# A hybrid attention and mixture-of-experts block: a longer hand-written order, with four small pieces of work moved in it

## The chip, the cores and the metric

The kernel runs on one core of a Trainium2 chip. The metric is the device time of one execution in microseconds (us). The engines are called PE (TensorE), DVE (VectorE), ACT (ScalarE), POOL (GpSimd) and SP (SyncE, which here issues nearly all DMAs). Each engine takes its instructions strictly in program order.

## What is computed

One decoder layer on 256 tokens of width 1024, in float32. A mixer comes first (an input projection, two kinds of attention, gates, an output projection), then a layer norm, then a mixture of 32 experts of which each token takes four.

```python
proj = x @ w_in + b_in                       # 4120 columns: q, k, v, gates
y_a = banded_attention(...)                  # sliding window 128, with sinks
y_b = nsa_attention(...)                     # g0*compressed + g1*selected + g2*window
gate_a, gate_b = jnp.split(jax.nn.sigmoid(merge_g), 2, axis=-1)
merged = gate_a * (y_a @ w_branch_a) + gate_b * (y_b @ w_branch_b)
h = layer_norm(alpha * x + merged @ w_out, ln1_g, ln1_b)
logits = h @ w_router + b_router             # top 4 of 32 experts, softmax
# each expert: act = clamped_swiglu(xb @ w_gate_up[e] + b_gate_up[e]); act @ w_down[e] + b_down[e]
out = layer_norm(alpha * h + moe(h), ln2_g, ln2_b)
```

## The kernel before

**The stages.** The mixer's input projection is 32 *units* of 128 columns. Unit 0 to 15 make queries, keys and values, unit 16 to 31 the merge gates (tiles `M`, `mg`). A unit is 24 matmuls (units 0 and 1: 8), because each operand is split into a high and a low part (`mm3`, lines 256 to 258), and runs as two *half units* of 12; half unit `h` belongs to unit `h // 2`. After the units come eight products with the branch weights (`pb`), the output projection (`po`), the router, and then the 32 experts, whose weights (12 MB each) stream from memory into some twelve 2 MB buffers. SP issues the next load into a buffer as soon as the readers of what it held are done.

**The order between half units.** After each half unit the main loop calls the steps that the table `PLAN` names for it. For an attention pair `br r` (two heads; branch 0, 1, 2) `S` makes the scores (PE, DVE, then ACT's exponentials for branches 1 and 2), `N` normalises them (DVE, then four operations on POOL, line 693), `T` transposes them (PE, then copies `pT` on ACT, line 705), and `V` multiplies with the values and adds to `yB` (line 727; for branch 2 ACT and DVE then make the high and low part `yhl`). `cp0` to `cp3` add the compressed branch, which reads `pcT`, the transposed compressed probabilities that step `ct` makes (`pct` on PE, a copy on ACT, line 604). `mlp`, `gelu` and `ck` make the compressed keys: a product `phid`, a copy `hp_`, a product `phidT`, a chain of six small operations on `cu` (lines 541 to 547, one of them ACT's tanh) and the product `pkc`. `h` and `l` make the high and low part of a unit's weights (`w_j`), two to three units ahead; the low part reads the high part. PE's transposes take their results from a pool of two PSUM buffers named `t`, PE's scores and `cp` products from three named `s`.

**Other steps.** `bl`, `bsa` to `bsd`, `bw` and `br` load the experts' biases, split them into three bfloat16 parts in a tile `bt` (lines 488 and 490, DVE and ACT), store them to a buffer `bd` in memory and load them again as rows `bparts`. `rw` scales the router's weights (lines 775 and 776, four DVE operations), sums them over partitions on PE (`pgb`, line 778) and adds the sums to constants. `sig` applies the sigmoid, in place, to the gates of the units from 16 to `SIG0 - 1`, which were copied out of PSUM without it; from unit `SIG0` on the copy applies it. `vt0` transposes a value tile.

**Who sets the order.** PE and SP run in program order throughout. DVE, ACT and POOL run in program order up to half unit `MAN_END`; what comes behind that is put in order by a scheduler, which may also take an instruction ahead. At half unit `END_H` (42) the attention's tiles are released, and expert weights load over them.

Of the kernel before, what the change touches and what calls it, by code (L numbers as in the profile page):

```python
# [10 lines left out]
F32 = mybir.dt.float32  # L11
# [9 lines left out]
P = 128  # L21
# [3 lines left out]
E = 32  # L25
# [7 lines left out]
GELU_C = math.sqrt(2.0 / math.pi)  # L33
NRA, NRB = 3, 3
WARM = 6
NWS, NSB, AHEAD, SIG0 = 3, 6, 2, 20
POOL_PART = {6: 'h', 8: 'h', 9: 'h', 10: 'h', 11: 'h', 12: 'h', 13: 'h', 14: 'h', 15: 'h', 16: 'h', 17: 'h', 18: 'h', 19: 'h', 20: 'h', 21: 'h', 22: 'h', 23: 'h', 24: 'h', 25: 'h', 27: 'l', 28: 'l', 30: 'l', 38: 'l'}
SIDE_R = "right"
LOADS, LOADS2 = 6, 11
# [3 lines left out]
MAN = 2  # L43
TWO = 4
LATE = range(6, 22)
MAN_END = 42
LN_ROWS = {9 + i: (0, i) for i in range(4)} | {20 + i: (1, i) for i in range(4)}
E_RES = 13
PLAN = {7: 'gates', 8: 'sinks blkz', 9: 'c1 gsum h6 l6', 10: 'S00 h7 l7 E00', 11: 'S01 h8 E01 N00', 12: 'vt0 S02', 13: 'N01 T00 E02 l8 h9', 14: 'N02 V00 T01 S03 bias1', 15: 'h10 V01 T02 E03', 16: 'l9 V02', 17: 'N03 l10 bl', 18: 'T03 h11 l11', 19: 'V03 blocks',
# [3 lines left out]
        43: 'sig', 44: 'sel'}  # L53
PRE = {26: 1, 43: 1, 45: 1, 48: 1, 64: 1, 71: 1, 72: 2, 73: 3}


# [8 lines left out]
def tile_block(ctx: ExitStack, tc: tile.TileContext, a, out):  # L65
# [4 lines left out]
    cp = ctx.enter_context(tc.tile_pool(name="cp", bufs=1))  # L70
# [134 lines left out]
    def w_tile(name):  # L205
        nw[0] += 1
        return ps_w.tile([P, 512], F32, tag=f"w{nw[0] % 2}", name=name)
# [8 lines left out]
    pp = er.enter_context(tc.tile_pool(name="pp", bufs=2, side=SIDE_R))  # L216
# [333 lines left out]
    hid = mp.tile([P, 2, 4, 32], F32, name="hid")  # L550
# [61 lines left out]
    def cmp_pv(r):  # L612
        t = ps_s.tile([P, 512], F32, tag="s", name=f"yc{r}")
        q_ = slice(32 * r, 32 * r + 32)
        for g in range(2):
            PE.matmul(t[64 * g:64 * g + 64, :S], vc[q_, 64 * g:64 * g + 64], y_["pcT"][q_, g, :], start=True, stop=True,
                      tile_position=(32 * r, 64 * g))
        DVE.tensor_tensor(y_["B"][:, r, :], y_["B"][:, r, :], t[:, :S], ALU.add)
# [145 lines left out]
    def sigmoids():  # L764
        for k in sorted((k for k in mg if 16 + k[0] + 2 * k[1] < SIG0), key=lambda k: (k[1], k[0])):
            ACT.activation(mg[k], mg[k], AF.Sigmoid)

    def router_weights():

        wb = pp.tile([P, 384], F32, tag="s", bufs=NSB, name="wb")[:, :256].rearrange("p (j e) -> p j e", j=NJ)  # L770
        gb = pp.tile([P, 384], F32, tag="s", bufs=NSB, name="gb")[:, :2 * E]
        for i in (1, 0):
            v = const[:, C_L1 + 8 * i:C_L1 + 8 * i + 8].unsqueeze(2).to_broadcast([P, NJ, E])
            w_ = wb if i else wr
            DVE.tensor_tensor(w_, wr, v, ALU.mult)
            DVE.tensor_reduce(gb[:, E * i:E * i + E], w_.rearrange("p j e -> p e j"), AX.X, ALU.add)
        t = ps_t.tile([P, 512], F32, tag="t", name="pgb")
        PE.matmul(t[:, :2 * E], ones, gb, start=True, stop=True)
        DVE.tensor_copy(wr_g, t[:, :E])
        DVE.tensor_tensor(br_b, br_b, t[:, E:2 * E], ALU.add)  # L780

    def sel():
# [4 lines left out]
    steps = {"bl": bias_load, "bsa": lambda: bias_split(0, "h"), "bsb": lambda: (bias_split(0, "l"), bias_split(1, "h")),  # L787
             "bsc": lambda: bias_split(1, "l"), "bsd": lambda: bias_split(2, "h"), "bw": bias_store, "br": bias_rows,
             "gates": gates, "gsum": gates_sum, "c1": load_c1, "sinks": sinks, "blkz": blocks_zero, "blocks": blocks, "mlp": mlp, "x": load_x, "gelu": gelu,
             "ck": ck, "hid": cmp_rows, "cv": cmp_v, "csm1": cmp_exp, "csm2": cmp_softmax, "ct": cmp_transpose, "rw": router_weights, "sig": sigmoids, "sel": sel}  # L790
    for b in range(3):
        steps[f"vt{b}"] = lambda b=b: v_transpose(b)
        steps[f"bias{b}"] = lambda b=b: load_T(b)
        for r in range(4):
            p = pairs[b][r]
# [4 lines left out]
    for r in range(4):  # L800
        steps[f"E0{r}"] = pa[r].exps
        steps[f"cp{r}"] = lambda r=r: cmp_pv(r)
    plan = {k: [steps[x] for x in v.split()] for k, v in PLAN.items()}
    h = 0
    for n in range(len(order)):
        for _ in unit(n):
            for f in plan.get(h, ()):
                f()
            if h == MAN_END:
                m0.close()  # L810
# [9 lines left out]
    for mt in range(8):  # L820
# [6 lines left out]
        t = w_tile(f"pb{mt}")  # L827
# [23 lines left out]
    lg = cp.tile([P, 2, 40], F32, name="lg")  # L851
    rep = cp.tile([P, 2, 40], F32, name="rep")
    sel = cp.tile([P, 2, E], F32, name="sel")
    gate = cp.tile([P, 2, E], F32, name="gate")
    posm = cp.tile([P, 2, E], F32, name="posm")
    v8 = cp.tile([P, 2, 8], F32, name="v8")
    sm = cp.tile([P, 2, 2], F32, name="sm")
# [363 lines left out]
    for e in range(E):  # L1221
        x, p = ex[e], (ex[e - 1] if e else None)
# [91 lines left out]
    with tc.For_i(0, nrun, 1) as e:  # L1314
# [13 lines left out]
        for tt in range(2):  # L1328
            t_ = slice(tt * P, (tt + 1) * P)
            for jj in range(2):  # L1330
                t = ps_w.tile([P, 512], F32, tag="w0", name=f"vht{tt}{jj}")
# [5 lines left out]
            for hf in range(2):  # L1337
# [7 lines left out]
                t = ps_w.tile([P, 512], F32, tag="w0", name=f"vt{tt}{hf}")  # L1345
# [116 lines left out]
```

## Time and profile before

| | |
|---|---|
| median of three runs | 1135.81 us (1134.64 to 1136.35) |
| profiled execution, its own time | 1137.99 us |
| its span, first to last instruction | 1136.2 us |
| mean granted PE clock | 0.988 |
| PE busy | 1067.2 us, 94% |
| DVE, ACT, POOL busy | 288.0, 212.2, 72.3 us |
| moved by DMA | 438.50 MB, mean 386 GB/s |

The span lies 1.8 us below the execution's own time, and that execution lies 2.2 us above the median of the runs. The page's chain of work follows only the last 0.1 us (a loop that runs zero times here), so the stages have to be read from tables by stretch, from timelines and from waits.

### The profile page before, as it was taken

The numbers are of one execution on the slowest core, as the hardware profiler recorded it, in microseconds if no ns is written. First come the engines' busy times: TensorE is split into PE (matmuls) and PEld (weight loads), VectorE is DVE, ScalarE is ACT, GpSimd is POOL, SyncE is SP. The second block draws the span as 40 slices with busy tenths as digits, with TensorE's granted clock in tenths as the row PEclk, the third lists the DMA queues.
The fourth block names the chain that finished last, engine by engine and source line by source line (L and its number), as shares of the span: only waits on it lengthen the run. The fifth ranks groups of instructions, "written<-read, shape, count | busy, mean of one in ns | idle before, by whom it ended". The sixth has DMA issues, their size and how long they took to land. (4 is left out here: it accounts for less than half of the span.)

```text
span 1136.2 us, 13443 instructions
## 1 busy us (share of the span) xinstructions
PE 1067.2 (94%) x5660; PEld 510.9 (45%) x5660; DVE 288.0 (25%) x695; ACT 212.2 (19%) x451; POOL 72.3 (6%) x113
## 2 busy tenths in 40 slices
PE   9999899999999999999999998998999988999995
PEld 7887798633434343434333433333433333333331
DVE  4885447412111111111121211111120202021213
ACT  3438344211101010111110101010111010001011
POOL 1444220000000000000000000000000000000000
PEclk9999899999999999999999999999999999999998
DMA  8654668799999999999999999999999999999993
GB/s 316 241 237 145 259 257 337 294 403 414 430 425 428 426 427 427 429 427 427 427 428 426 428 427 426 430 424 429 427 428 427 427 427 426 428 428 427 427 428 145
DMA packets 38288, 438.50 MB, mean 386 GB/s; under 512 B 4032, under 2 KB 6736, under 8 KB 9168
## 3 DMA queue, kind: packets, MB, share of 16 engines
q1 hardware_dynamic: 37888, 436.98, 92.2%
q8 instruction: 46, 0.75, 0.3%
q10 hardware_dynamic: 336, 0.62, 0.2%
q14 instruction: 18, 0.15, 0.0%
HBM read 435.92 MB, written 1.66 MB: 385 GB/s over the span
## 5 line engine op out<-in xcount | busy, mean ns | idle before, releaser
L1169 PE MATMUL g<-wg,xeM 128*64 128x512 f32 x1208 | 278.7, 598 | 2.9 <-DMA wg<-in_w_gu_dram 2.8
L1169 PEld LDWEIGHTS g<-wg,xeM 128*64 128x64 f32 x1208 | 82.4, 137 | 155.1 <-issue 136.1
L1196 PE MATMUL pd<-wd,wk 128*64 128x512 f32 x600 | 134.8, 595 | 16.8 <-DMA wd<-in_w_d_dram 16.7
L1169 PE MATMUL g<-wb,xeM 128*64 128x512 f32 x624 | 143.9, 596 | 1.2 <-DMA wb<-in_w_gu_dram 1.2
L1203 DVE COPY y<-pd 64x512 f32<-64x512 f32 x32 | 22.2, 694 | 432.8 <-ACT y L1202 432.8
L1196 PEld LDWEIGHTS pd<-wd,wk 128*64 128x64 f32 x600 | 43.0, 137 | 102.7 <-issue 79.8
L1149 DVE TENSOR_SCALAR gs<-g 128x512 f32<-128x512 f32 x32 | 22.1, 692 | 240.8 <-PE g L1169 240.8
L1169 PEld LDWEIGHTS g<-wb,xeM 128*64 128x64 f32 x624 | 42.6, 137 | 80.8 <-issue 72.7
L1196 PE MATMUL pd<-wb,wk 128*64 128x512 f32 x288 | 66.5, 608 | 9.2 <-DMA wb<-in_w_d_dram 9.1
L1202 ACT COPY y<-pd 64x512 f32<-64x512 f32 x32 | 18.5, 579 | 295.5 <-PE pd L1196 295.5
L256 PE MATMUL pu<-xhl,w_j 128*128 128x256 f32 x240 | 72.6, 302 | 0.3 <-ACT kT L436 0.2
L257 PE MATMUL pu<-xhl,w_j 128*128 128x256 f32 x240 | 69.2, 288 | 0.0
L258 PE MATMUL pu<-xhl,w_j 128*128 128x256 f32 x240 | 69.1, 288 | 0.0
L1124 PEld LDWEIGHTS px<-wk,h_tok 128*128 128x128 f32 x480 | 55.8, 191 | 24.3 <-issue 12.2
L1083 POOL TENSOR_SCALAR wk<-const,posm 128x64 f32<-128x64 f32 x30 | 12.8, 446 | 796.3 <-PE pst L1138 792.2
L1124 PE MATMUL px<-wk,h_tok 128*128 128x128 f32 x480 | 61.5, 281 | 0.0
L1145 PE MATMUL yac<-y,wk 128*128 128x512 f32 x128 | 59.2, 605 | 0.7 <-ACT y L1202 0.7
L1185 ACT COPY wk<-pa 128x512 f32<-128x512 f32 x31 | 18.2, 587 | 196.9 <-PE pa L1184 185.6
L256 PEld LDWEIGHTS pu<-xhl,w_j 128*128 128x128 f32 x240 | 47.3, 197 | 4.0 <-issue 2.7
L1169 PE MATMUL g<-wp,xeM 128*64 128x512 f32 x208 | 48.4, 596 | 0.0
L257 PEld LDWEIGHTS pu<-xhl,w_j 128*128 128x128 f32 x240 | 47.4, 198 | 0.0
L258 PEld LDWEIGHTS pu<-xhl,w_j 128*128 128x128 f32 x240 | 47.3, 197 | 0.1
(246 smaller groups left out, 1018.6 us busy)
## 6 DMA issues: line engine op xcount, KB each, us to landing
wg<-in_w_gu_dram SPq DMA_DIRECT2D x72, 2048.0 KB, 38.5
wb<-in_w_gu_dram SPq DMA_DIRECT2D x38, 2048.0 KB, 34.5
wd<-in_w_d_dram SPq DMA_DIRECT2D x36, 2048.0 KB, 39.1
wb<-in_w_d_dram SPq DMA_DIRECT2D x16, 2048.0 KB, 39.1
wp<-in_w_gu_dram SPq DMA_DIRECT2D x12, 2048.0 KB, 38.2
w<-in_w_in_dram SPq DMA_DIRECT2D x14, 1024.0 KB, 7.6
wp<-in_w_d_dram SPq DMA_DIRECT2D x7, 2048.0 KB, 39.1
wg<-in_w_gu_dram SPq DMA_DIRECT2D x7, 1024.0 KB, 10.3
```

The source lines that it names most:

```text
L256: PE.matmul(o_, wh, xh, start=start, stop=False)
L257: PE.matmul(o_, wh, xl, start=False, stop=False)
L258: PE.matmul(o_, wl, xh, start=False, stop=stop)
L1083: (DVE if tt else POOL).tensor_scalar(oh[:, tt, k, :], iota[:, :CAP], posm[:, tt, e + k:e + k + 1], None, ALU.is_equal)
L1124: PE.matmul(t[:, k * P:(k + 1) * P], h_tok[:, tt, j * P:(j + 1) * P], oh[:, tt].rearrange("p k s -> p (k s)"), start=(tt == 0), stop=(tt = ...
L1145: PE.matmul(yac[tt][o_], st[:, tt * P:(tt + 1) * P], y2[:, o_, :], start=first, stop=last)
L1149: DVE.tensor_scalar_min(g_, gate_, LIMIT)
L1169: PE.matmul(self.g[b][64 * hf:64 * hf + 64, :], xes[e][:, j, :], w[:, 1024 * b + 512 * hf:1024 * b + 512 * hf + 512], start=False, stop=(j ...
L1185: ACT.copy(self.aT, t)
L1196: PE.matmul(d[64 * o_:64 * o_ + 64, :], self.aT[:, P * j + 64 * hf:P * j + 64 * hf + 64], w[j // 2][:, 1024 * (j % 2) + 512 * o_:1024 * (j ...
L1202: ACT.copy(y2[k, 0, :], d[:CAP])
L1203: DVE.tensor_copy(y2[k, 1, :], d[CAP:])
```

## The change

`MAN_END` goes from 42 to 50, so that the hand-written order holds for eight half units more, and with it nine things change place:

- `sig` from half unit 43 to 48, for eight gates rather than four (`SIG0` 24), so units 20 to 23 are copied out without the sigmoid;
- `bsb`, `bsc`, `bsd`, `bw` and `br` from half units 21, 22, 26, 28 and 35 to 35, 36, 37, 38 and 42;
- `rw` is cut in two: the DVE part, `rwd`, at half unit 41, the sum on PE, `rwp`, at 47 (before both were at 42). Its result now stands in the tile `gate`, which lives to the end, and not in a tile of the attention's pool;
- `ct` ahead of `S21`, and `vt0` behind `S02`, within their half units.

```diff
-NWS, NSB, AHEAD, SIG0 = 3, 6, 2, 20
+NWS, NSB, AHEAD, SIG0 = 3, 6, 2, 24
...
-MAN_END = 42
+MAN_END = 50
...
-        20: 'h12 l12 bsa', 21: 'bsb mlp', 22: 'h13 bsc gelu', 23: 'ck l13', 24: 'S10 h14', 25: 'h15 l14 N10 hid', 26: 'S11 bsd', 27: 'T10 l15 N11 h16 S12',
...
-        43: 'sig', 44: 'sel'}
...
+        20: 'h12 l12 bsa', 21: 'mlp', 22: 'h13 gelu', 23: 'ck l13', 24: 'S10 h14', 25: 'h15 l14 N10 hid', 26: 'S11', 27: 'T10 l15 N11 h16 S12',
...
+        44: 'sel', 47: 'rwp', 48: 'sig'}
...
+    gate = cp.tile([P, 2, E], F32, name="gate")
+    gb = gate.rearrange("p t e -> p (t e)")
+
     def router_weights():
 
         wb = pp.tile([P, 384], F32, tag="s", bufs=NSB, name="wb")[:, :256].rearrange("p (j e) -> p j e", j=NJ)
-        gb = pp.tile([P, 384], F32, tag="s", bufs=NSB, name="gb")[:, :2 * E]
         for i in (1, 0):
             v = const[:, C_L1 + 8 * i:C_L1 + 8 * i + 8].unsqueeze(2).to_broadcast([P, NJ, E])
             w_ = wb if i else wr
             DVE.tensor_tensor(w_, wr, v, ALU.mult)
             DVE.tensor_reduce(gb[:, E * i:E * i + E], w_.rearrange("p j e -> p e j"), AX.X, ALU.add)
+
+    def router_sums():
         t = ps_t.tile([P, 512], F32, tag="t", name="pgb")
         PE.matmul(t[:, :2 * E], ones, gb, start=True, stop=True)
         DVE.tensor_copy(wr_g, t[:, :E])
```

On ACT, at step `S21`, before. The scheduler had taken the four sigmoids of `sig` (line 766) ahead to between the pairs of branch 2, each with a table load on either side (`M` is a gate, `sb_1` the pair's scores, `pct` the transposed compressed probabilities):

```order
L705 COPY pT_3_0_1165<-t_3_0_1161 128x384
L705 COPY pT_3_1_1171<-t_3_1_1167 128x384
L766 ACT_TABLE_LOAD
L766 ACTIVATE M_72<-M_72 128x256
L679 ACT_TABLE_LOAD
L679 ACTIVATE sb_1_0_1207,su_1_1206<-sb_1_0_1207,st_1_1205 128x256
...
L604 COPY pcT<-pct 128x512
L459 ACTIVATE M_74<-pu_1180,const 128x256
```

and now, at the same place:

```order
L705 COPY pT_3_0_1161<-t_3_0_1157 128x384
L705 COPY pT_3_1_1167<-t_3_1_1163 128x384
L604 COPY pcT<-pct 128x512
L679 ACTIVATE sb_1_0_1210,su_1_1209<-sb_1_0_1210,st_1_1208 128x256
...
L459 ACTIVATE M_74<-pu_1176,const 128x256
```

The sigmoid and both table loads are gone from here, and the copy of `pcT` stands ahead of the exponentials. The eight sigmoids with one table load stand behind the high part of unit 26's weights, ahead of the copy of unit 24's gate.

On DVE, at steps `mlp`, `gelu` and `ck`, before (`bt` is the biases' tile, `hp_`, `cx` and `cu` are the small chain's):

```order
L432 TENSOR_SCALAR qT_665<-pu_684,pk 128x256
L490 TENSOR_TENSOR bt<-bt 128x768
L531 COPY hp__749<-phid 128x128
L490 TENSOR_TENSOR bt<-bt 128x768
L541 COPY cx<-phidT 128x60
L542 TENSOR_TENSOR cu<-cx 128x60
```

and now:

```order
L432 TENSOR_SCALAR qT_666<-pu_685,pk 128x256
L531 COPY hp__748<-phid 128x128
L541 COPY cx<-phidT 128x60
L542 TENSOR_TENSOR cu<-cx 128x60
L543 TENSOR_TENSOR cu<-cu,cx 128x60
```

The two passes over the biases are gone from ahead of the chain. They stand in the pairs of branch 2 now: one behind `N21`'s two operations and ahead of `S22`'s, one behind `cp0` and the low part of unit 20's weights, and the cast `bsd` ahead of `S23`'s.

On DVE, at step `V23` (the last pair), before (`w_j22` and `w_j23` are units 22's and 23's weights, `yB` and `yhl` as above, `const_66` holds the router's weights):

```order
L234 TENSOR_TENSOR w_j22_1431<-w10_681,w_j22_1431 128x1024
L727 TENSOR_TENSOR yB_751<-yB_751,y2_2_1447 128x256
L234 TENSOR_TENSOR yhl_167<-yB_751,yhl_167 128x256
L234 TENSOR_TENSOR w_j23_1481<-w10_681,w_j23_1481 128x1024
L727 TENSOR_TENSOR yB_751<-yB_751,y2_3_1497 128x256
...
L775 TENSOR_TENSOR wb_1507<-const_66 128x256
L776 TENSOR_REDUCE gb_1508<-wb_1507 128x32
L775 TENSOR_TENSOR const_66<-const_66 128x256
L776 TENSOR_REDUCE gb_1508<-const_66 128x32
L779 COPY const_66<-pgb_1513 128x32
```

and now:

```order
L234 TENSOR_TENSOR w_j22_1431<-w10_682,w_j22_1431 128x1024
L727 TENSOR_TENSOR yB_750<-yB_750,y2_2_1447 128x256
L234 TENSOR_TENSOR yhl_167<-yB_750,yhl_167 128x256
L777 TENSOR_TENSOR wb_1480<-const_66 128x256
L778 TENSOR_REDUCE gate_170<-wb_1480 128x32
L777 TENSOR_TENSOR const_66<-const_66 128x256
L778 TENSOR_REDUCE gate_170<-const_66 128x32
L234 TENSOR_TENSOR w_j23_1486<-w10_682,w_j23_1486 128x1024
L727 TENSOR_TENSOR yB_750<-yB_750,y2_3_1502 128x256
```

The router's four operations stand ahead of unit 23's low part and of `V23`'s addition. PE's product `pgb` stood right behind `V23`'s products, ahead of the second half of unit 21; now it stands behind unit 23. On SP the store to `bd` and the load of `bparts` move behind the last two loads of the input weights, and `bparts` behind the load of `x` as well.

## Rows read from the trace of the kernel before

**Rows 1.** Stretches: us; PE, PEld, DVE, ACT, POOL busy (count); PE clock, DMA share, GB/s.

```profile
128.00:216.00 88.00, 87.70 (x658) 82.56 (x658) 47.40 (x87) 37.92 (x54) 13.43 (x10) 0.98 0.78 309
216.00:260.00 44.00, 43.60 (x222) 17.35 (x220) 10.22 (x33) 6.75 (x13) 0.00 (x0) 1.00 0.96 386
...
400.00:1000.00 600.00, 566.07 (x2702) 219.67 (x2700) 98.50 (x213) 72.08 (x145) 8.55 (x20) 0.99 1.01 427
```

**Rows 2.** SP's waits, 216 to 262 us: waited for, us in total, times, longest.

```profile
SPq L83 <- PE g L1169: 26.7, 11, 8.3
```

**Rows 3.** Timeline of PE: start, us, line, names, shapes, count, [idle before, releaser].

```profile
33.32 0.44 PE L472 MATMUL pvt<-const,vt 128*128 128x128 f32 x2 [1.28 <-ACT vt L440]
...
63.75 0.40 PE L561 MATMUL pkc<-cu,pk 128*64 128x15 f32 x4 [2.11 <-DVE cu L547]
...
99.18 0.30 PE L700 MATMUL t<-const,sb 128*128 128x128 f32 x1 [1.98 <-ACT pcT L604]
...
111.78 0.33 PE L700 MATMUL t<-const,sb 128*128 128x128 f32 x1
...
121.72 1.50 PE L718 MATMUL y<-pT,V 128*64 128x256 f32 x4 [2.17 <-ACT pT L705]
...
127.05 0.66 PE L778 MATMUL pgb<-gb,const 128*128 128x64 f32 x2 [3.40 <-DVE gb L776]
```

**Rows 4.** Stretches at and behind three of these gaps, columns as in rows 1.

```profile
63.75:67.00 3.25, 3.25 (x18) 2.99 (x18) 1.55 (x3) 0.00 (x0) 0.00 (x0) 0.50 0.41 169
...
99.18:102.60 3.42, 3.42 (x28) 2.74 (x28) 0.58 (x5) 2.93 (x6) 1.60 (x4) 1.00 1.02 343
121.71:131.90 10.19, 6.77 (x31) 6.01 (x32) 4.07 (x10) 1.22 (x3) 1.05 (x1) 0.50 0.83 328
```

**Rows 5.** Timeline of DVE at the small chain.

```profile
60.10 0.96 DVE L490 TENSOR_TENSOR bt<-bt 128x768 f32<-128x768 f32 x1 [0.70 <-ACT bt L488]
...
61.73 1.09 DVE L544 SCALAR_TENSOR_TENSOR cu<-cu,cx 128x60 f32<-128x60 f32 x1
```

**Rows 6.** Timeline of POOL.

```profile
61.72 1.05 POOL L226 TENSOR_SCALAR w_j<-w 128x1024 fp32r<-128x1024 f32 x1 [3.33 <-DVE cu L543]
...
108.56 1.64 POOL L693 TENSOR_SCALAR sb<-sb,su 128x256 f32<-128x256 f32 x4 [2.77 <-DVE su L690]
115.42 1.63 POOL L693 TENSOR_SCALAR sb<-sb,su 128x256 f32<-128x256 f32 x4 [5.22 <-DVE su L690]
117.02 2.07 POOL L226 TENSOR_SCALAR w_j<-w 128x1024 fp32r<-128x1024 f32 x2
...
141.25 2.40 POOL L232 TENSOR_TENSOR w_j<-w,w_j 128x1024 fp32r<-128x1024 f32 x1 [6.15 <-ACT w_j L228]
```

**Rows 7.** ACT, 92 to 117 us, grouped: count, busy us, mean ns, idle before.

```profile
L766 ACT ACT_TABLE_LOAD x4 | 5.1, 1283 | 0.1
...
L766 ACT ACTIVATE M<-M 128x256 f32<-128x256 f32 x4 | 1.7, 419 | 0.0
```

**Rows 8.** Timeline of ACT.

```profile
121.20 0.85 ACT L705 COPY pT<-t 128x384 f32<-128x384 f32 x2
...
139.76 0.48 ACT L461 ACTIVATE M<-pu,const 128x256 f32<-128x256 f32 x1 [1.47 <-PE pu L258]
...
142.64 0.48 ACT L461 ACTIVATE M<-pu,const 128x256 f32<-128x256 f32 x1 [1.47 <-PE pu L258]
```

**Rows 9.** Timeline of DVE at the last pair.

```profile
118.10 2.06 DVE L234 TENSOR_TENSOR w_j<-w,w_j 128x1024 fp32r<-128x1024 f32 x1 [2.85 <-POOL w_j L226]
120.08 0.41 DVE L727 TENSOR_TENSOR yB<-yB,y 128x256 f32<-128x256 f32 x1
...
124.92 0.42 DVE L775 TENSOR_TENSOR wb<-const 128x256 f32<-128x256 f32 x1
...
126.32 0.58 DVE L776 TENSOR_REDUCE gb<-const 128x32 f32<-128x256 f32 x1
```

**Rows 10.** DMA issues, whole span: KB each, us from issue to landing.

```profile
bd<-bt SPq DMA_DIRECT2D x1, 576.0 KB, 15.2
```

More of the change, by code (lines that the diff above doesn't have):

```diff
@@ L45 @@
 LATE = range(6, 22)
-MAN_END = 42
+MAN_END = 50
 LN_ROWS = {9 + i: (0, i) for i in range(4)} | {20 + i: (1, i) for i in range(4)}
 E_RES = 13
-PLAN = {7: 'gates', 8: 'sinks blkz', 9: 'c1 gsum h6 l6', 10: 'S00 h7 l7 E00', 11: 'S01 h8 E01 N00', 12: 'vt0 S02', 13: 'N01 T00 E02 l8 h9', 14: 'N02 V00 T01 S03 bias1', 15: 'h10 V01 T02 E03', 16: 'l9 V02', 17: 'N03 l10 bl', 18: 'T03 h11 l11', 19: 'V03 blocks',
[3 rows of a table removed]
-        43: 'sig', 44: 'sel'}
+PLAN = {7: 'gates', 8: 'sinks blkz', 9: 'c1 gsum h6 l6', 10: 'S00 h7 l7 E00', 11: 'S01 h8 E01 N00', 12: 'S02 vt0', 13: 'N01 T00 E02 l8 h9', 14: 'N02 V00 T01 S03 bias1', 15: 'h10 V01 T02 E03', 16: 'l9 V02', 17: 'N03 l10 bl', 18: 'T03 h11 l11', 19: 'V03 blocks',
[3 rows of a table added]
+        44: 'sel', 47: 'rwp', 48: 'sig'}
 PRE = {26: 1, 43: 1, 45: 1, 48: 1, 64: 1, 71: 1, 72: 2, 73: 3}
@@ L789, in tile_block @@
              "gates": gates, "gsum": gates_sum, "c1": load_c1, "sinks": sinks, "blkz": blocks_zero, "blocks": blocks, "mlp": mlp, "x": load_x, "gelu": gelu,
-             "ck": ck, "hid": cmp_rows, "cv": cmp_v, "csm1": cmp_exp, "csm2": cmp_softmax, "ct": cmp_transpose, "rw": router_weights, "sig": sigmoids, "sel": sel}
+             "ck": ck, "hid": cmp_rows, "cv": cmp_v, "csm1": cmp_exp, "csm2": cmp_softmax, "ct": cmp_transpose, "rwd": router_weights, "rwp": router_sums, "sig": sigmoids, "sel": sel}
     for b in range(3):
@@ L853, in tile_block @@
     sel = cp.tile([P, 2, E], F32, name="sel")
-    gate = cp.tile([P, 2, E], F32, name="gate")
     posm = cp.tile([P, 2, E], F32, name="posm")
```

4 rows, old and new, of the table PLAN are left out of this document.

## The prediction

> **What bounds the kernel now.** I read the table by stretches first, because the chain of work says nothing here. From 400 to 1000 us the DMA engines are busy throughout at 427 GB/s and PE has 34 us of idle time in 600: the weight stream sets the pace. From 128 to 216 us it is the other way round: PE is busy 87.70 of 88.00 us and DMA stands at 0.78 [rows 1]. The two meet at 216 us. There SP's waits say who lets the stream go: eleven loads, 26.7 us in all, wait for PE's products `g` of the first expert to read a buffer empty [rows 2]. Up to then the buffers are full and the stream has to stand still; from then on the remaining bytes take a fixed time. So the end moves by as much as PE's arrival at the first expert moves, and since PE never waits between 128 and 216 us, that is PE's gain up to 128 us, one for one. What the experts do afterwards is the same program.
>
> Up to 128 us the timeline of PE shows five gaps at places that the change touches: 1.28 us at 33.32, 2.11 at 63.75, 1.98 at 99.18, 2.17 at 121.72 and 3.40 at 127.05 [rows 3]. Behind two of them the granted clock fell to 0.50, that is from 2.4 to 1.2 GHz: from 63.75 to 67.00 and from 121.71 to 131.90 us. Behind the 1.98 us at 99.18 it stayed at 1.00 [rows 4].
>
> **The change, part by part.**
>
> *The router's sum, `rw`.* `pgb` stands ahead of unit 21's second half, and PE waits 3.40 us for it [rows 3], because its four DVE operations (two of 0.42, two of 0.58) can begin only when DVE has done `V23` [rows 9]. Now the product is asked for behind unit 23, and the operations stand ahead of `V23`'s: **3.4** gained. Cover for the moved part: its 2.0 us on DVE delay unit 23's low part, which is wanted 1.5 units after `V23`, 4.3 us at the 2.88 us from one gate copy to the next [rows 8]. Nothing is lost.
>
> *The last pair's gap, 2.17 us.* PE waits for ACT's `pT`, done from 121.20 on [rows 8]. Backwards from it: ACT waits for `V22`'s addition on DVE (120.08), which stands behind unit 22's low part (118.10, 2.06), which needs its high part from POOL (117.02), which stands behind `N23`'s normalisation (115.42, 1.63) [rows 6, 9]. `N23` follows the pair's exponentials, ahead of which a table load of 1.28 us goes [rows 7]. So the chain comes 1.28 us earlier against PE, and up to 0.8 more if the low part is no longer slowed by POOL, which works beside it. The gap falls to between 0.1 and 0.9; I take 0.6, gain **1.6** (bounds 1.3 and 2.1).
>
> *The clock behind it.* In 121.71 to 131.90 PE was busy 6.77 us at half rate [rows 4]; at full rate that is **3.4** less. It comes if both gaps ahead go (bounds 0 and 3.4). I take all of it: 1.98 us of idle time did not cost the clock, and at most 0.9 is left.
>
> *`ct` ahead of `S21`.* The second transpose of `T20` needs the `t` buffer that `pct` holds until ACT has copied `pcT`, and that copy stood behind a sigmoid, two table loads and four exponentials. Now it stands ahead of them: the 1.98 us go, **2.0** (bounds 1.3, if ACT were still busy by one load's length, and 2.0). `S21` comes a product later, but its exponentials lose a table load, and that is more.
>
> *The biases' passes leave the small chain.* The pass at 60.10 held DVE for 0.96 us ahead of the chain that PE waits for. The chain then met POOL: an operation on 60 columns began at 61.73 and took 1.09 us, until POOL's high part (61.72, 1.05) had ended [rows 5, 6]. Started 0.9 us sooner, that operation escapes, but a later one of the chain can meet the same POOL operation. Gain between 0.8 and 1.7 of the 2.11; I take **1.2**. The clock: 3.25 us busy at half rate [rows 4], **1.6** (bounds 0 and 1.6), since about 0.9 us of gap is left.
>
> Here the Trainium skill speaks against the change. The row shows DVE waiting out POOL's operation [rows 5, 6]. The page "SBUF — State Buffer", section "SBUF: two separate sides", states that DVE (in some modes, or with two SBUF inputs) and POOL share a port pair that whoever starts first locks for its whole instruction; the trace agrees in this row. By that rule the same passes, now right behind `N21`'s two operations, can shut POOL out just as it should normalise: that is a rival below.
>
> *Where the passes go.* DVE gets 0.96 us twice and a cast, ACT one cast, in the pairs of branch 2. The cover: `N22`'s normalisation ends at 110.20, `T22` wants it at 111.78 [rows 3, 6], 1.6 us of slack, to which the lost table load adds 1.28. I cost it at nothing; without the cover it would be about 1 us at each of two pairs.
>
> *`vt0` behind `S02`.* `S02` fills part of the 1.28 us that PE waits for ACT's value tile. What follows hangs on exponentials that do not move, so not all of it lasts: **0.6** (bounds 0 and 1.28, half of it).
>
> *The eight sigmoids at half unit 48.* No table load and eight of 0.42 are left: 1.28 + 3.35 = 4.6 us on ACT [rows 7] between the high part of unit 26 and the copy of unit 24's gate. Queued behind: that copy, the high part of unit 27, and POOL's low part of it (2.40 us, from 141.25 to 143.65 [rows 6]), which unit 27 wants at 142.64 + 2.88 = 145.52 [rows 8]. The bundle starts where unit 26's high part ends, one period before 141.2, at 138.3, and ends at 142.9 instead of the copy's start at 139.76: 3.1 us of delay against 1.9 of slack, a loss of 1.2 at most. Instructions of one kind overlap a little on ACT, and `pgb` gives PE some tenths of its own there, so the other bound is 0.1; I take a loss of **0.5**.
>
> On the load itself the rows show 1.28 us and the next activation right behind. The Trainium skill, page "ScalarE: Activation LUTs", section "What ACT_TABLE_LOAD costs", adds a drain of 1.38 us to each switch, 2.66 together. The trace shows no such pause, and by the page's figure the loss would be 1.9 us and the time 1.4 us later than mine.
>
> *SP.* The store `bd` now waits for the last cast, with the `w_br` loads behind it, which wait longer anyway, for unit 23's low part. A store took 15.2 us to land [rows 10], and `bparts`, asked for some 15 us later, may hold the queue for a few us; the expert loads behind it are first read beyond 216 us. Nothing.
>
> **The sum.** 3.4 + 1.6 + 3.4 + 2.0 + 1.2 + 1.6 + 0.6 - 0.5 = 13.3 us. Against the profiled execution's 1137.99 that is 1124.7; the median of the runs lies 2.2 us below it, so I expect 1135.8 - 13.3 = **1122.5 us**.
>
> **The rivals.**
>
> *A gap stays long enough for the clock to fall* (0.13). For it: the three gaps near 2 us differ by 0.2 us, and only two cost the clock. Then the last pair's 1.6 and the 3.4 are lost: gain 8.3, 1127.5 us. The gap at 63.75 is the smaller case, with 1.6 us lost inside my range.
>
> *The port rule bites* (0.06): the biases' passes shut POOL out at `N21` and `N22`, each for 0.96 us, and the casts delay the exponentials by as much. It decides once the delay exceeds the 2.9 us of slack. Two waits of 1.5 us cost 3: 1125.5; with a fall of the clock as above some 1129.
>
> *Hidden anyway* (0.05). If the stream and not PE set the start, a buffer earlier would be no byte earlier: about 1135.8. Against it stand the DMA share of 0.78 from 128 to 216 us and SP's waits for PE.
>
> *Slower* (0.03). The clock: if new waits in the pairs of branch 2 kept PE at half rate, each busy microsecond there would cost half of one. To pass the bound on the far side it has to eat 13.3 + 2.3 us, 31 us at half rate, nearly all of the stretch from 92 to 128: about 1138 or more. Nothing in the rows holds it down that long; the longest fall was 10.2 us.
>
> *The drain of the page on ScalarE* (0.03): 1123.9.
>
> **How the numbers follow.** My forecast has 0.70, with a range of its own of 1120.5 (all upper bounds together gain about 15) to 1125. The range for 8 in 10 reaches from 1120.0, half a microsecond of the runs' scatter lower, to 1127.5, the first rival. A measurement of this kernel can tell about 0.2%, 2.3 us, from no change. Faster than that are my forecast, the first two rivals and the last, 0.92; within it the hidden case, 0.05; slower 0.03.
>
> **What would show it.** The timeline of PE without waits over 1 us at `T20`, `V23` and `pkc`, and with unit 21's second half right behind `V23`; a granted clock of 1.00 from 60 to 140 us; ACT without a table load between the pairs and with one ahead of eight activations near 125 us; SP's first waits for the products `g` some 13 us sooner than 216 us, and everything behind shifted by the same. A clock of 0.5 behind `V23`, or waits of PE at `T21` or `T22`, would make me wrong by 3 to 5 us; the first `g` 13 us sooner with the same end would refute the way the gain is carried.

## The result and the profile after

The kernel after takes 1123.74 us (median of five runs, 1122.8 to 1124.51) against 1135.81 us before (five runs, 1134.64 to 1137.78). The ratio is 0.9893, with a 95% interval from 0.9879 to 0.9908: 12.1 us faster, where 13.3 were forecast. A second comparison (experiment 12) gave 1123.57 us for the kernel after and 1138.32 us for the kernel before beside it, a ratio of 0.9878 (0.9862 to 0.9895): 14.8 us. The median of the kernel before lies between 1135.81 and 1138.32 us from one comparison to the next, so the times alone put the gain at 12 to 15 us.

The timeline of PE after, at the places of [rows 3] and at the first expert:

```profile
33.75 0.44 PE L472 MATMUL pvt<-const,vt 128*128 128x128 f32 x2
...
61.36 0.29 PE L561 MATMUL pkc<-cu,pk 128*64 128x15 f32 x4 [0.45 <-DVE cu L547]
...
93.28 0.27 PE L700 MATMUL t<-const,sb 128*128 128x128 f32 x1
...
113.81 0.81 PE L718 MATMUL y<-pT,V 128*64 128x256 f32 x3 [0.39 <-ACT pT L705]
114.99 0.38 PE L256 MATMUL pu<-xhl,w_j 128*128 128x256 f32 x1
...
122.27 0.33 PE L782 MATMUL pgb<-gate,const 128*128 128x64 f32 x2
...
201.88 0.65 PE L1172 MATMUL g<-wp,xeM 128*64 128x512 f32 x2
```

Of the five gaps of [rows 3], three are gone (1.28, 1.98 and 3.40 us), one has shrunk from 2.11 to 0.45 us and one from 2.17 to 0.39. One wait stands in no bracket, since it lies inside a group: from V23's first product to unit 21's next it takes 1.18 us (113.81 to 114.99), where 0.80 do without a wait (112.36 to 113.16 in experiment 11). V23 needs both of ACT's copies `pT`, and together they last until 114.15, as the timeline of ACT after shows:

```profile
113.30 0.85 ACT L705 COPY pT<-t 128x384 f32<-128x384 f32 x2
```

Stretches after, with columns as in [rows 1]; the first two answer to [rows 4], the last two to [rows 1]:

```profile
61.36:64.61 3.25, 3.25 (x28) 2.88 (x29) 2.16 (x6) 0.00 (x0) 0.76 (x1) 1.00 0.90 373
...
113.81:124.00 10.19, 10.19 (x83) 9.72 (x84) 6.62 (x13) 3.09 (x7) 2.09 (x2) 1.00 0.60 236
...
128.00:202.00 74.00, 73.64 (x554) 68.37 (x554) 44.50 (x83) 34.92 (x50) 11.29 (x8) 1.00 0.87 345
202.00:246.00 44.00, 43.60 (x222) 17.32 (x224) 10.22 (x33) 6.87 (x13) 0.00 (x0) 1.00 0.96 386
```

The granted clock is 1.00 behind both places. From V23 on, PE did 83 products in 10.19 us where it did 31 in [rows 4]. SP's waits from 200 to 250 us (waited for, us in total, times, longest) read as [rows 2] did from 216 to 262, word for word but for the line number:

```profile
SPq L83 <- PE g L1172: 26.7, 11, 8.3
```

So the whole pattern at the meeting of mixer and weight stream has moved with PE: the first expert's first product stood at 215.74 us and stands at 201.88, 13.9 us sooner, and the span has gone from 1136.2 to 1122.4 us.

**Where the time went, by stretches.** Each column below is the time on PE from the first product named to the next one: S03's scores, `pkc`, S10's scores, S20's scores, V23, the first `pb`, the first expert's `g`, the end. All fourteen traces of this study are in it, under the labels of their runs; every kernel but the first two and `sigmoids_alone` is the kernel after, with one edit or none.

```
kernel            S03 at  S03-pkc pkc-S10 S10-S20 S20-V23 V23-pb  pb-g   S03-g   g-end
before             39.92   23.83    3.19   20.35   34.43   38.00  56.02  175.82  920.5
before_again       39.70   23.81    1.85   20.37   34.42   38.17  56.00  174.63  921.0
after              39.41   21.95    1.84   20.29   30.32   32.04  56.03  162.47  920.5
after_again        38.80   21.97    1.84   20.37   30.32   32.04  56.01  162.56  922.0
router_sum_back    39.42   21.96    1.84   20.38   30.31   38.48  56.02  169.00  920.4
ct_back            38.97   21.98    1.85   20.38   31.19   32.06  56.01  163.47  922.5
biases_back        37.75   23.63    2.33   21.41   30.21   32.04  56.00  165.61  920.7
sigmoids_back      38.16   21.97    1.84   20.37   35.40   31.73  56.03  167.34  921.1
vt0_back           38.13   22.22    1.84   20.37   30.32   32.06  56.02  162.84  920.9
t23_ahead          38.42   21.96    1.85   20.38   30.06   31.68  57.31  163.23  921.0
sigmoids_alone     38.44   23.82    1.84   20.37   31.06   38.30  56.03  171.41  920.8
two_loads_more     38.02   21.98    1.84   20.38   30.34   36.15  56.03  166.73  921.1
pe_work_expert10   39.31   21.98    1.84   20.31   30.36   32.06  56.02  162.57  920.4
l22_behind_v22     38.32   21.96    1.85   20.37   29.87   31.67  56.02  161.73  920.5
```

From S03 to the first expert an undisturbed stretch repeats within 0.1 us, so an edit shows there to the tenth. The scatter between executions lies at both ends: in where S03 stands (37.75 to 39.92 us) and from the first expert to the end (920.4 to 922.5 us).

### The profile page after: what moved, and what is told of

Read it like the earlier page. It is cut to its first block, busy times and chain, and to the rows that moved or that the text cites. A ratio compares the mean times of both kernels' runs of the same rounds, so it can differ in the third digit from the quotient of the medians.

```text
span 1122.4 us, 13451 instructions
## 1 busy us (share of the span) xinstructions
PE 1063.6 (95%) x5660; PEld 507.4 (45%) x5660; DVE 287.8 (26%) x695; ACT 204.9 (18%) x449; POOL 74.8 (7%) x113
## 3 DMA queue, kind: packets, MB, share of 16 engines
HBM read 435.92 MB, written 1.66 MB: 390 GB/s over the span
## 5 line engine op out<-in xcount | busy, mean ns | idle before, releaser
L256 PE MATMUL pu<-xhl,w_j 128*128 128x256 f32 x240 | 71.1, 296 | 0.2 <-ACT kT L436 0.2
L258 PE MATMUL pu<-xhl,w_j 128*128 128x256 f32 x240 | 67.8, 282 | 0.1
L257 PE MATMUL pu<-xhl,w_j 128*128 128x256 f32 x240 | 67.7, 282 | 0.0
L256 PEld LDWEIGHTS pu<-xhl,w_j 128*128 128x128 f32 x240 | 45.7, 191 | 4.1 <-issue 2.8
L258 PEld LDWEIGHTS pu<-xhl,w_j 128*128 128x128 f32 x240 | 45.7, 191 | 0.3 <-POOL w_j L232 0.3
L257 PEld LDWEIGHTS pu<-xhl,w_j 128*128 128x128 f32 x240 | 45.8, 191 | 0.0
```

The source lines that it names most:

```text
L256: PE.matmul(o_, wh, xh, start=start, stop=False)
L257: PE.matmul(o_, wh, xl, start=False, stop=False)
L258: PE.matmul(o_, wl, xh, start=False, stop=stop)
```

## The experiments

Of the long lines of `PLAN` the diffs show only the entries that change. A ratio stands against the runs of the kernel before that were made beside it.

**1. The kernel before, a second time.** No edit.

> The kernel before, unchanged, for a second trace and for what no change looks like in a comparison. In the two traces at hand PE's first product of the first expert moved from 215.74 to 201.88 us, 13.9 us, while the medians differ by 12.1; the profiled execution of before lay 2.2 us above its median. If the scatter between executions lies in the mixer, this trace has another arrival at the first expert, by about as much as its span differs from 1136.2 us. If it lies in the weight stream, the arrival is 215.7 again (within 0.3) and only what follows differs. The ratio should be 1.000 within 0.002.

Measured: 1135.81 us, ratio 0.9993 (0.9982 to 1.0004). The arrival is 214.32 us, 1.4 us sooner, and the span 0.9 us shorter (from the first expert to the end it takes 0.5 us more). Of the earlier arrival only 0.2 us come from the start (S03); the rest lies at one place in the mixer. The gap of 2.11 us at `pkc` is there again, and behind it the clock is 1.00, where it was 0.50 in [rows 4]; the stretch behind V23 shows 0.51 again. Timeline of PE, and then stretches with columns as in [rows 1]:

```profile
63.51 0.29 PE L561 MATMUL pkc<-cu,pk 128*64 128x15 f32 x4 [2.11 <-DVE cu L547]
```

```profile
63.51:66.76 3.25, 3.25 (x28) 2.88 (x29) 1.95 (x6) 0.00 (x0) 0.00 (x0) 1.00 0.40 164
...
120.16:130.30 10.14, 6.74 (x30) 5.98 (x31) 4.03 (x10) 1.20 (x3) 1.04 (x1) 0.51 0.86 334
```

The same gap costs the clock in one execution and not in another. From S03 to the first expert the change is therefore worth 13.3 us (175.82 to 162.5) or 12.1 (174.63 to 162.5), and the medians, 12.1 apart, may be a mixture of such executions; which of the runs without a trace paid for the clock is not known.

**2. The router's sum put back.**

```diff
-        41: 'T23 rwd', 42: 'V23 x br',
-        44: 'sel', 47: 'rwp', 48: 'sig'}
+        41: 'T23', 42: 'V23 x rwd rwp br',
+        44: 'sel', 48: 'sig'}
```

> The kernel after, with the router's four DVE operations and the product behind unit 21's first half again. My theory: PE waits 3.0 to 3.4 us for the product again, and the first expert starts as much later, at about 205 us. What the clock does tells two readings apart. If it was the 2.17-us gap that cost the clock in the kernel before, and that gap stays away here (0.39 us), then either the 3-us gap costs it too (another 1.7 us, 5.0 in all, some 1128.7 us) or it doesn't (3.2 in all, some 1127.0). Rival, hidden anyway: 1123.7, no change.

Measured: 1129.81 us, ratio to before 0.9940 (0.9927 to 0.9954). Timeline of PE, and the stretch behind:

```profile
118.57 0.44 PE L782 MATMUL pgb<-gate,const 128*128 128x64 f32 x1 [3.40 <-DVE gate L778]
```

```profile
118.57:124.97 6.40, 6.40 (x30) 6.40 (x31) 1.60 (x4) 0.47 (x1) 1.04 (x1) 0.51 1.04 400
```

The wait is 3.40 us to the hundredth, and the clock falls behind it although the gap at V23 is only 0.38 us here. From V23 to the branch products 6.4 us more: 3.4 of wait and 3.0 of clock, where I had expected at most 1.7 of clock. Undoing this one step takes back half of the whole gain. The clock's part is not this step's alone: in [rows 4] the clock was down already behind V23's gap, before the wait for the product, and in experiment 6, where V23's gap is all but gone and the 3.40 us stay, nothing is gained from V23 to the branch products. The rival that the gain is hidden anyway is out.

**3. The compressed probabilities' transpose put back.**

```diff
-        34: 'N20 ct S21 l19',
+        34: 'N20 S21 ct l19',
```

> The kernel after, with the compressed probabilities' transpose behind S21 again. By my prediction this place alone is worth 2.0 us: PE waits about 2 us at T20's second transpose, first expert near 203.9 us, 1125.7 us in all. Rival: the wait came from the sigmoid and the two table loads that stood ahead of the copy on ACT, and with them gone the copy ends some 0.5 us behind the time that T20 wants it; the gap is 0.3 to 0.7 us, the time 1124.2. The clock stays at 1.00 in both.

Measured: 1124.94 us, 0.9896 (0.9881 to 0.9911). Timeline of PE:

```profile
93.79 0.30 PE L700 MATMUL t<-const,sb 128*128 128x128 f32 x1 [0.70 <-ACT pcT L604]
```

The gap is 0.70 us and not 2, and S20 to V23 takes 0.9 us more. The rival holds: the larger part of the 1.98 us came from the sigmoid and the loads ahead of the copy, not from the place of `ct`.

**4. The biases' steps put back.**

```diff
-        21: 'mlp', 22: 'h13 gelu', 26: 'S11', 28: 'vt1',
+        21: 'bsb mlp', 22: 'h13 bsc gelu', 26: 'S11 bsd', 28: 'vt1 bw',
...
-        35: 'V13 T20 h20 N21 bsb', 36: 'S22 cp0 l20 bsc', 37: 'V20 T21 cp1 h21 N22 bsd', 38: 'S23 cp2 l21 bw', 42: 'V23 x br',
+        35: 'V13 T20 h20 N21 br', 36: 'S22 cp0 l20', 37: 'V20 T21 cp1 h21 N22', 38: 'S23 cp2 l21', 42: 'V23 x',
```

> The kernel after, with all steps of the biases at their old places. My theory: the gap ahead of pkc is 2.1 us again (0.45 now) and the clock falls to 0.50 for some 3.2 us behind it: 1.7 and 1.4 to 1.6 us, first expert near 205.1 us, 1126.9 us in all. If the clock holds, 1.7 us alone. Rival: what the passes cost in the pairs of branch 2 (POOL's first normalising operation of N21 takes 1.05 us beside one of them) is on the path, and comes back there: then the loss is 2.5 us or less, and a gap in the pairs is smaller than in the kernel after.

Measured: 1127.03 us, 0.9914 (0.9901 to 0.9928). From S03 to the first expert 3.1 us more: 1.66 ahead of `pkc` (23.63 less 21.97), and 1.5 of clock behind it (0.5 up to S10, 1.0 up to S20). Timeline of PE, and the stretch behind:

```profile
61.38 0.29 PE L561 MATMUL pkc<-cu,pk 128*64 128x15 f32 x4 [2.11 <-DVE cu L547]
```

```profile
61.38:65.40 4.02, 4.02 (x25) 3.27 (x25) 1.55 (x3) 0.00 (x0) 0.00 (x0) 0.65 0.32 130
```

S20 to V23 is 0.1 us shorter without the passes, so among the pairs of branch 2 they cost next to nothing. They do collide with POOL there. The timelines of DVE (the two passes) and POOL (N21's four operations, and a high part) in the kernel after:

```profile
94.26 0.96 DVE L490 TENSOR_TENSOR bt<-bt 128x768 f32<-128x768 f32 x1
98.86 1.79 DVE L490 TENSOR_TENSOR bt<-bt 128x768 f32<-128x768 f32 x1
...
94.51 2.20 POOL L693 TENSOR_SCALAR sb<-sb,su 128x256 f32<-128x256 f32 x4 [0.50 <-DVE su L690]
98.42 1.43 POOL L226 TENSOR_SCALAR w_j<-w 128x1024 fp32r<-128x1024 f32 x1 [1.72 <-PE pu L258]
```

POOL's operations, 1.63 us in [rows 6], take 2.20 beside the first pass, and the second pass takes 1.79 us instead of 0.96: POOL's operation ends at 99.85, and the pass 0.80 us behind that. That is the lock of the Trainium skill's page "SBUF — State Buffer", section "SBUF: two separate sides", and these rows agree with it, in both directions. The slack absorbed it: PE waits for neither.

**5. The sigmoids put back between the pairs.**

```diff
-NWS, NSB, AHEAD, SIG0 = 3, 6, 2, 24
+NWS, NSB, AHEAD, SIG0 = 3, 6, 2, 20
...
-MAN_END = 50
+MAN_END = 42
...
-        44: 'sel', 47: 'rwp', 48: 'sig'}
+        43: 'sig', 44: 'sel', 47: 'rwp'}
```

> The kernel after, with the sigmoid on four gates behind half unit 43 and the hand-written order up to 42 again, so that the scheduler takes the four sigmoids ahead, each with table loads, between the pairs of branch 2. My theory: N23's exponentials and with them POOL's and DVE's parts of the chain come 1.1 to 1.3 us later against PE, and the gap at V23 grows from 0.39 us to between 1.5 and 2.2. If the clock holds, 1.3 to 1.8 us are lost, some 1125.3 us in all; if it falls behind the gap as in the kernel before, 3 us more, some 1128. T20 waits 0 to 0.3 us, since the copy of the compressed probabilities stands ahead of the second table load. Rival, the loads between the pairs were covered and the gap at V23 came from POOL beside DVE alone: gap under 1.2 us, 1124.4 or less.

Measured: 1128.02 us, 0.9914 (0.9899 to 0.9928); 4.9 us more from S03 to the first expert. Timelines: two waits of PE, and ACT and DVE at the first of them; then the stretches behind the two:

```profile
104.28 0.43 PE L616 MATMUL yc<-pcT,vc 32*64 32x256 f32 x2 [2.52 <-DVE yB L618]
...
117.74 0.43 PE L718 MATMUL y<-pT,V 128*64 128x256 f32 x1 [2.18 <-DVE wb L777]
...
101.43 1.28 ACT L766 ACT_TABLE_LOAD   x1
102.73 0.42 ACT L766 ACTIVATE M<-M 128x256 f32<-128x256 f32 x1
103.05 0.39 ACT L228 CAST yhl<-yB 128x256 fp32r<-128x256 f32 x1
...
103.47 0.43 DVE L234 TENSOR_TENSOR yhl<-yB,yhl 128x256 fp32r<-128x256 f32 x1 [3.31 <-ACT yhl L228]
103.81 0.41 DVE L618 TENSOR_TENSOR yB<-yB,yc 128x256 f32<-128x256 f32 x1
```

```profile
104.28:107.50 3.22, 3.22 (x26) 2.39 (x27) 3.15 (x14) 1.12 (x1) 1.79 (x4) 1.00 0.49 176
117.74:127.90 10.16, 10.16 (x83) 9.69 (x84) 6.32 (x11) 2.98 (x6) 2.09 (x2) 1.00 0.62 237
```

The gap at V23 is in the range that I gave, at its upper end (the releaser named there, `wb`, is not read by the product; the first of its `pT` copies on ACT ended within 0.1 us of the same time). My theory missed the other one. ACT's high part of `yhl` stands behind a load and a sigmoid; DVE's low part waits 3.31 us for it, and behind that on DVE's queue stands the addition that frees the `s` buffer that PE wants for `cp2`. The kernel before, with the same loads but the biases' passes and their cast on ACT elsewhere, has no such gap; the scheduler also put that sigmoid at another place there, and no run tells the two apart. And the clock stayed at 1.00 behind gaps of 2.52 and 2.18 us. That the time meets the 1128 us that I gave for a fall of the clock is luck: the second wait cost about what the clock did not.

**6. The sigmoids' move alone.** The kernel before with:

```diff
-NWS, NSB, AHEAD, SIG0 = 3, 6, 2, 20
+NWS, NSB, AHEAD, SIG0 = 3, 6, 2, 24
...
-MAN_END = 42
+MAN_END = 50
...
-        43: 'sig', 44: 'sel'}
+        44: 'sel', 48: 'sig'}
```

> The kernel before, with one part of the change: the hand-written order up to half unit 50 and the sigmoid of eight gates behind 48. My theory: with the four sigmoids and their table loads gone from between the pairs, T20 waits 0.7 us instead of 1.98 and V23 0.4 instead of 2.17, with no other part of the change; 3.40 us at the router's product and 2.11 at pkc stay. From S20's first product to V23 it takes 31.2 us (34.4 in before, 30.3 in after), from V23 to the branch products 38.5, as with the router's sum alone put back. About 2.8 us better than before, some 1133. Rival, by my prediction's sum: T20's 1.98 us stay, since they were booked to the place of the compressed probabilities' transpose, and only the 1.6 at V23 go.

Measured: 1132.9 us, 0.9965 (0.9951 to 0.9979). Timeline of PE:

```profile
62.26 0.29 PE L561 MATMUL pkc<-cu,pk 128*64 128x15 f32 x4 [2.11 <-DVE cu L547]
...
95.09 0.30 PE L700 MATMUL t<-const,sb 128*128 128x128 f32 x1 [0.71 <-ACT pcT L604]
...
115.52 0.43 PE L718 MATMUL y<-pT,V 128*64 128x256 f32 x1 [0.27 <-ACT pT L705]
...
120.17 0.45 PE L778 MATMUL pgb<-gb,const 128*128 128x64 f32 x1 [3.40 <-DVE gb L776]
```

All as expected: 0.71 us left at T20, 0.27 at V23, and 31.06 us from S20 to V23. The rival, that all of T20's wait belongs to `ct`, falls a second time; the 0.71 us left are what `ct`'s place takes. The 2.11-us gap did not cost the clock in this execution (1.84 us from `pkc` to S10); the 3.40-us gap did (38.30 from V23 to `pb`).

**7. The value transpose put back.**

```diff
-        12: 'S02 vt0',
+        12: 'vt0 S02',
```

> The kernel after, with the first value transpose ahead of S02 again. My theory: PE waits 1.28 us for it; from the first S00 product to the first S03 product it takes 12.9 us instead of 12.4, the gap of 0.44 us at 45 us becomes 0.64, and the first expert comes 0.7 us later relative to S00: some 1124.4 us. Rival: 1.28 us, all of the wait, 1125.0; or nothing, since everything behind hangs on exponentials that don't move.

Measured: 1123.95 us, 0.9880 (0.9862 to 0.9898). The wait is not 1.28 us but 0.17, in the timelines of ACT and PE:

```profile
24.89 1.03 ACT L228 CAST w_j<-w 128x1024 fp32r<-128x1024 f32 x1
...
31.41 0.33 PE L472 MATMUL pvt<-const,vt 128*128 128x128 f32 x1 [0.17 <-ACT vt L440]
```

In the second trace of before, with 1.28 us again, ACT's cast of a weight waits for a load to land, and ACT's work behind it comes later against PE:

```profile
26.17 1.05 ACT L228 CAST w_j<-w 128x1024 fp32r<-128x1024 f32 x1 [0.59 <-DMA w<-in_w_in_dram]
...
33.11 0.44 PE L472 MATMUL pvt<-const,vt 128*128 128x128 f32 x2 [1.28 <-ACT vt L440]
```

In the first trace of before, with 1.28 us too, the cast waits 0.41 us for its load; in `sigmoids_alone`, with `vt0` ahead as well, it waits for none, and PE's timeline shows no wait for `vt0`. From S00 to S03 it takes 11.5 to 12.9 us in the executions of both orders (12.89, 12.88, 11.54 and 11.90 with `vt0` ahead; 11.45 to 12.89 without), so no gain is shown there. Behind S03 the transpose's place costs 0.25 us up to `pkc`. My theory of 0.7 falls; 0.2 to 0.3 is what the traces hold.

**8. Two loads more in the bundle.**

```diff
+    sm_x = cp.tile([P, 8], F32, name="sm_x")
+    POOL.memset(sm_x, 0.0)
+
     def sigmoids():
...
             ACT.activation(mg[k], mg[k], AF.Sigmoid)
+            if k == (1, 1):
+                ACT.activation(sm_x, sm_x, AF.Exp)
```

> The kernel after, with an exponential on a scratch tile of 8 columns between the fourth and the fifth of the eight sigmoids, so two table loads more on ACT. It prices the bundle's cover. In the trace after, unit 27's third product starts 0.34 us behind the second where 0.12 is the pitch: POOL's low part of unit 27, held up by the bundle, came 0.2 us late, so no slack is left. My theory: the bundle grows by 2.7 to 2.9 us and PE waits about that long ahead of unit 27, one for one; the first expert 2.7 us later relative to the products ahead, some 1126.5 us. With a slack of 1.9 us, as my prediction had it, 1 us, some 1124.7. By the drain that the Trainium skill's page on ScalarE states (page ScalarE: Activation LUTs, section What ACT_TABLE_LOAD costs), 2.8 us more than mine, with a pause of over 1 us behind each load.

Measured: 1127.94 us, 0.9918 (0.9901 to 0.9934). Timelines of ACT and PE, and the stretch behind:

```profile
122.64 1.28 ACT L769 ACT_TABLE_LOAD   x1
123.94 1.34 ACT L769 ACTIVATE M<-M 128x256 f32<-128x256 f32 x4
125.28 1.28 ACT L771 ACT_TABLE_LOAD   x1
126.58 0.21 ACT L771 ACTIVATE sm_x<-sm_x 128x8 f32<-128x8 f32 x1
126.80 1.28 ACT L769 ACT_TABLE_LOAD   x1
...
129.84 0.39 PE L256 MATMUL pu<-xhl,w_j 128*128 128x256 f32 x1 [2.69 <-ACT M L461]
```

```profile
129.84:133.30 3.46, 3.46 (x17) 3.46 (x18) 0.00 (x0) 2.19 (x3) 2.49 (x2) 0.55 1.00 412
```

The bundle grew by 2.9 us (from its first load to the copy behind it 6.70 us, against 3.77 in the kernel after) and PE waits 2.69, ahead of unit 26 and not of unit 27: nearly one for one, so there was next to no slack. By the releaser it waits for a buffer that a gate's copy (line 461) frees, not for POOL's low part as I had thought. The clock fell behind this gap, for 1.4 us more (36.15 less 32.04 is 4.1). Behind each of the three loads the next activation starts 0.02 us later: no drain as on the Trainium skill's page "ScalarE: Activation LUTs", section "What ACT_TABLE_LOAD costs".

**9. More work for PE in expert 10.**

```diff
+            if e == 10 and j == 6:
+                t = ps_w.tile([P, 512], F32, tag="w0", name="pextra")
+                for _ in range(8):
+                    PE.matmul(t, ones, const[:, :512], start=True, stop=True)
```

> The kernel after, with eight more products of 128x512 on PE in expert 10, which nothing reads. It tests whether the weight stream sets the pace there. My theory: from the first expert's first product to the end it takes 920.4 to 922.5 us, as in the ten traces so far, the time is 1123.7, and the work eats idle time of PE. Rival: PE sets the pace there too, and the time grows by as much as the eight products take, 2 to 7 us.

Measured: 1123.87 us, 0.9883 (0.9867 to 0.9898). The eight products, two instructions each, held PE from 481.1 to 488.2 us, 7.1 us, and from the first expert to the end it took 920.4 us. The view of their tile, and the stretch of the experts with columns as in [rows 1]:

```profile
L1245 PE MATMUL pextra<-const x16: 592/592/696, 481.1 to 487.6; 128*128 128x512 f32 x16
...
400.00:1000.00 600.00, 570.48 (x2708) 221.57 (x2708) 99.93 (x219) 70.02 (x141) 8.55 (x20) 0.99 1.01 427
```

PE is idle for 29.5 us of the stretch, against 34.8 in the kernel after, and the stream still moves 427 GB/s. These 7.1 us of PE work behind the first expert were free; work ahead of the first expert is paid in full, as the last column of the table shows for all the others.

**10. T23 ahead of V22.**

```diff
-        40: 'V22', 41: 'T23 rwd',
+        41: 'T23 V22 rwd',
```

> The kernel after, with T23 ahead of V22 and both behind half unit 41, so that ACT copies the last pair's transposes ahead of the high part of V22's result. My theory: the copies end before 113.4 us of the trace after, V23 waits neither for the first (0.39 us) nor for the second (0.4), and the first expert comes 0.8 us sooner relative to the products ahead: some 1123.0 us, which timing alone can hardly tell from the kernel after. Rival: V22's products, now behind the transposes, wait for something themselves, and nothing is gained.

Measured: 1124.44 us, 0.9885 (0.9868 to 0.9902). V23 waits no more, and up to the branch products 0.6 us are gained (S20-V23 and V23-pb). Then 1.3 us are lost in a stage that the edit does not touch: the scheduler, which orders what lies behind half unit 50, set two multiplications by gates (line 838) ahead of a low part on DVE, and PE waits at two places in its timeline, 0.65 of the 1.3 us (the rest shows as no single wait):

```profile
158.01 0.39 PE L258 MATMUL pb<-yhl,w_j 128*128 128x256 f32 x1 [0.30 <-DVE w_j L234]
...
162.69 0.36 PE L256 MATMUL pb<-yhl,w_j 128*128 128x256 f32 x1 [0.35 <-ACT w_j L228]
```

**11. Unit 22's low part behind V22.**

```diff
-LATE = range(6, 22)
+LATE = range(6, 23)
...
-        39: 'V21 T22 cp3 N23', 40: 'V22',
+        39: 'V21 T22 cp3 N23 h22', 40: 'V22 l22',
```

> The kernel after, with the low part of unit 22's weights on DVE behind V22's addition and low part instead of ahead of them. My theory: the addition, the high part on ACT and with it ACT's copies for V23 come about 1.8 us sooner; V23 waits neither for the first copy (0.39 us) nor for the second (0.4), and the stage of the branch products stays as it is: from S03's first product to the first expert 161.8 us instead of 162.5, some 1123.0 us, too little for the times alone to tell. Rival: unit 22's low part now comes too late, and PE waits ahead of unit 22.

Measured: 1122.43 us, 0.9877 (0.9861 to 0.9893), 161.73 us from S03 to the first expert. Timeline of PE:

```profile
112.36 0.65 PE L718 MATMUL y<-pT,V 128*64 128x256 f32 x4
...
113.16 0.39 PE L256 MATMUL pu<-xhl,w_j 128*128 128x256 f32 x1
```

The gap at V23 is gone, and the second copy's wait too: 0.74 us better than the kernel after by the trace. The intervals of the times overlap, so they cannot tell the two apart.

**12. The kernel after, a second time.** No edit.

> The kernel after, unchanged, for a second trace beside the other kernels. The gaps at pkc, V23 and behind are the same (0.45, 0.39 us), the clock stays at 1.00 up to the experts, and from S03's first product to the first expert it takes 162.5 us again within 0.2. What differs lies ahead of S03, where PE waits for the first weights: up to 2 us. Median 1123.7 within 1.

Measured: 1123.57 us, 0.9878 (0.9862 to 0.9895); 162.56 us from S03 to the first expert, against 162.47. S03 stands 0.6 us sooner, and the stretch behind the first expert is 1.5 us longer: here the scatter lies ahead and behind.

## Why the prediction was right, point by point

The forecast of 1122.5 us lies 1.2 us below the median, inside the range. Its way of carrying the gain holds: every edit moved the end by what it moved PE's arrival at the first expert, within the 2 us by which the stream scatters, and 7.1 us of work behind that point moved nothing. Term by term, the sizes from the traces of before and after:

| term | forecast | measured | from |
|---|---|---|---|
| router's sum | 3.4 | 3.4 | gap gone; 3.40 again when put back |
| last pair's gap | 1.6 | 1.4 | 2.17 to 0.39, less 0.38 for the second copy |
| clock behind it | 3.4 | 3.2 to 3.3 | V23-pb 5.96 to 6.13 shorter, less 3.40, plus the 0.38 and the 0.22 below |
| T20's gap (`ct`) | 2.0 | 2.3 | S20-V23 4.11 shorter, less 1.78 at V23 |
| gap at `pkc` | 1.2 | 1.7 | 2.11 to 0.45 |
| clock behind it | 1.6 | 1.35 or 0 | pkc-S10, by execution |
| `vt0` behind S02 | 0.6 | 0.2 | S03-pkc 1.87 shorter, less 1.66 |
| the bundle | -0.5 | -0.2 | timeline below |
| sum | 13.3 | 13.3 or 12.0 | S03-g: 13.35 or 12.07 |

That the larger sum meets the forecast to the tenth is luck: the terms miss by up to 0.5 us, in either direction, and the misses cancel. Of the 2.3 us at T20 the gap itself is 1.98; the other 0.3 are put down to no wait.

*What was mis-sized: the clock at `pkc`.* I put all of 1.6 us into the sum, from one trace; my lower bound of 0 stood for a gap that stays too long, not for a kernel before that keeps its clock. In four executions with that gap of 2.11 us the clock fell in two (`before`, `biases_back`) and held in two (`before_again`, `sigmoids_alone`). If half of all executions pay them, the 1.35 us are 0.7, over half of the 1.2 us between forecast and median. Four traces do not prove that share, and the 1.2 us are smaller than the 2.5 by which the median of before moves between comparisons.

*What was put in the wrong place: `ct`.* Its 2.0 us hold as a sum with the sigmoids. Alone, the sigmoids' leaving takes 1.98 to 0.71, and `ct`'s place the last 0.7 to 0.9. My lower bound of 1.3 was a slip: 1.98 us less a load's 1.28 leave 0.7. The chain that I read backwards at V23 had the same loads in it, and I should have booked both waits to them.

*What had too much cover: the bundle.* I gave it 1.9 us of slack and 4.6 us of length. Its length is 3.86, since the eight activations overlap, and its slack is next to nothing: experiment 8 paid 2.69 of 2.9 us. That the two errors nearly cancelled is luck. In the kernel after it costs unit 27's third product 0.22 us (the pitch is 0.12), in the timelines of ACT and PE below; from V23 to `pb` the run without the bundle there, `sigmoids_back`, is 0.31 us shorter.

```profile
123.90 1.28 ACT L766 ACT_TABLE_LOAD   x1
125.19 2.57 ACT L766 ACTIVATE M<-M 128x256 f32<-128x256 f32 x8
127.67 0.45 ACT L461 ACTIVATE M<-pu,const 128x256 f32<-128x256 f32 x1
...
131.25 0.28 PE L257 MATMUL pu<-xhl,w_j 128*128 128x256 f32 x1
131.59 0.38 PE L258 MATMUL pu<-xhl,w_j 128*128 128x256 f32 x1
```

*What was right with its condition: the passes among the pairs.* I costed them at nothing because the loads leave. Experiment 5 takes that condition away, and a wait of 2.52 us appears; how much of it is the passes' doing is not shown, since the scheduler's order differs there too.

*What was too high: `vt0`.* Its 1.28 us went with a weight's late landing: in the two traces where ACT's cast waited for the load (0.41 and 0.59 us) PE waited 1.28, in the two where the load was there 0.17 and nothing.

*The rivals.* A longer gap with the clock: no, 0.39 us. The port rule: it acted (0.57 us on POOL, 0.83 on DVE) and decided nothing. Hidden anyway, slower, the drain: none occurred.

## What to carry to other kernels

Find the point where the stage bound by compute hands over to the one bound by the stream: what moves the compute engine's arrival there is paid in full, what lies behind may be free (7.1 us here). Before you book a wait to a step's place in the queue, list everything that stands ahead of it and ask which part leaves by another edit; here undoing one part alone, and doing one part alone, gave 0.7 where 2.0 had been booked. A cost that depends on the clock is priced from several executions, not from one trace.

## What the runs showed of the hardware

- The length of a gap does not tell by itself whether the clock falls. It held behind 1.98 us (twice), 2.18 and 2.52; it fell behind 2.17 (twice), 2.69 and 3.40 (twice, not counting the two traces of before, where it was down already); behind 2.11 it did either, two and two. What decides stays open; no run here was made for it.
- Eight activations of 128x256 behind one another took 2.57 us, 0.32 each, where one alone took 0.42 [rows 7].
- The start of a program scatters and its waits absorb part of it: S00's first product stood between 25.4 and 28.0 us, S03's between 37.75 and 39.9. With `vt0` behind S02 the way from S00 to S03 was 11.45 us in the three executions with S00 behind 26.8 us, and 12.4 to 12.9 in the others; with `vt0` ahead no such order shows (S00 at 26.8, 26.9 and 27.0 us, and 12.9, 11.5 and 12.9 us from there).
